# Bank pairs, joined sums and a second group by sevens in a two-layer hybrid block kernel

## The chip, the cores and the metric

One core of a Trainium2 chip runs the kernel. The metric is the device time of one execution in microseconds (us), the median of several runs.

## The reference

A network of two layers works on 256 tokens of width 2048, all in float32. Each layer has a mixer and a gated feed-forward part with 5632 hidden columns; a last normalisation ends it.

```python
def swiglu(hn, w_gate, w_up, w_down):
    return (jax.nn.silu(hn @ w_gate) * (hn @ w_up)) @ w_down

def reference(x, ...):
    h = x
    for layer in range(DEPTH):
        if layer % 2 == 0:
            h = h + gdn_rglru_mixer(rmsnorm(h, ab_norm[j]), ...)
        else:
            h = h + fox_moba_mixer(rmsnorm(h, cd_norm[j]), ...)
        h = h + swiglu(rmsnorm(h, ffn_norm[layer]), ffn_w_gate[layer], ffn_w_up[layer], ffn_w_down[layer])
    return rmsnorm(h, final_norm)
```

The change touches the two feed-forward parts and the places where they meet the mixers and the last normalisation.

## The kernel before

**Products in three.** Every float32 operand is split into a high half (a cast on ScalarE, L179 for weights, L376 for sums of weights) and a low half (a subtraction on VectorE, L180 and L377), and a product is three matmuls: high by high, low by high, high by low (`Bank.add`, L409 to L411; `xstat`, L303 to L305). A matmul has 128 tokens as its stationary side and 512 output columns. X is the transposed input of a stage, `hid` the transposed hidden tiles, both kept as two halves.

**Blocks.** `block()` computes two groups of 512 output columns (i = 0, 1) for two token halves (t = 0, 1) into four PSUM banks `F[t][i]`. The depth is walked in groups of four k-tiles of 128. A group is done plainly, in 48 matmuls with four weight units of 128x1024, or "by sevens" (`seven()`, Strassen's scheme with Winograd's sums): seven products of six matmuls, 42 in all, on sums of the weights (`total()`, L384, split by `halves()`) and on combinations of the input (`combine()`, tile `comb`). Four of the seven go into four banks M, and `ends()` (L460 to L465) adds those up into four tiles `e`, which are added to F at the block's end. Products by sevens are spread between the plain ones.

**Feed-forward.** `ffn()` goes through the eleven pairs of gate and up columns in pieces of four, four and three blocks. A gate and up block ends with `e <- F, e` sums (L529, L533), a Silu on ScalarE (L530) and a scaled product on VectorE (L534). `turn()` transposes such hidden tiles inside the next block (`Ph`, L503) and splits them into `hid` (L507, L508). After each piece come two down blocks (p = 0, 1) on `hid`, whose results go into the residual `h` (L554, L561). Gate and up blocks do two groups by sevens, except the first of each layer, which does none; the down blocks of the pieces of four do one for p = 0 and two for p = 1, those of the piece of three one each. A `hooks` table names the work that is put in at a plain product's number: the transposes, the combinations, a norm.

**Seams.** `phase()` opens the SBUF pools of a stage. The PSUM pools `acc` (four tiles of one bank; `Px` of the mixers and `F` share it) and `msp` (four tiles; `M`, transposes `Pt`, `Ph`) are opened once. A mixer ends with `out_proj()`, which adds `Px` to `h` (L359) and transposes it to X (`to_x()`, L326 to L328); the second mixer starts with projections `Px` on X by `xstat()`. The last block of the program sums up under `fin` (L557): `second_half()` takes the four `add` calls, sums of squares on ScalarE (L317), means (L1159), a root (L1164) and rates (L1168 to L1170), and writes the output; there VectorE's and ScalarE's order is as written. Elsewhere the scheduler sets it from the program's order and from the tiles' dependences. Each engine works through its own instructions in order.

## Time and profile before

| | |
|---|---|
| runs | 2228.13, 2226.42, 2227.39 us; median 2227.39 |
| profiled execution | 2228.4 us, span 2226.6 us |
| TensorE clock granted | 0.999 of full |
| TensorE busy | 2211.8 us, 99% |
| VectorE busy | 1917.1 us, 86% |
| ScalarE busy | 1284.9 us, 58% |
| GpSimd busy | 50.6 us, 2% |
| feed-forward of layer 0 | from 432 to 1128 us |
| feed-forward of layer 1 | from 1525 us to the end |

Matmuls are pipelined: one takes 0.39 us from start to end, and the next one starts well before that end. So the pitch of a row of matmuls is read from their starts. The same holds on VectorE in part: a new instruction starts a little before the last one ends.

### The profile page before, as it was taken

The page shows a single profiled execution, that of the slowest core. Times are in us where ns is not written, and L with a number is a line of the kernel's source. Part 1 is how long each engine was busy: PE and PEld are TensorE (multiplying, and loading weights), DVE is VectorE, ACT ScalarE, POOL GpSimd, SP SyncE. Part 2 cuts the span into 40 slices and gives each one's busy share as a digit, 9 for nine tenths or more (in the row PEclk, how much of TensorE's full clock was granted, in tenths as well). Part 3 has the DMA queues.
Part 4 walks back from the last instruction along what each step waited for, and adds up shares of the span by engine and source line. Part 5 has one row for each costly group of instructions (what it writes and reads, how often), then busy time and mean ns, then how long its engine had stood idle before and what let it go on. Part 6 is the DMA issues. An engine that isn't in the chain of part 4 may idle for free.

```text
span 2226.6 us, 30372 instructions
## 1 busy us (share of the span) xinstructions
PE 2211.8 (99%) x11002; PEld 1847.0 (83%) x11002; DVE 1917.1 (86%) x2713; ACT 1284.9 (58%) x1687; POOL 50.6 (2%) x62
## 2 busy tenths in 40 slices
PE   9999999999999999999999999999999999999998
PEld 8888888888888888888878888888888888888886
DVE  8899676679999999999966658866999999999998
ACT  6776664555555665555654444545665566555565
POOL 0000000000000000000000000000000000000000
PEclk9999999999999999999999999999999999999999
DMA  7445445677777776777665455556777777777774
GB/s 281 155 146 163 141 152 184 208 223 227 212 227 231 220 233 211 225 230 225 193 196 171 161 169 175 168 178 185 223 226 216 221 225 238 219 214 239 218 236 151
DMA packets 125992, 451.67 MB, mean 203 GB/s; under 512 B 14065, under 2 KB 15601, under 8 KB 125713
## 3 DMA queue, kind: packets, MB, share of 16 engines
q1 hardware_dynamic: 117488, 420.10, 58.3%
q0 software_dynamic: 8064, 29.36, 7.8%
q8 instruction: 86, 1.41, 0.3%
q14 instruction: 66, 0.53, 0.1%
q10 hardware_dynamic: 288, 0.27, 0.0%
HBM read 447.58 MB, written 2.10 MB: 202 GB/s over the span
## 4 chain that ended last, share of the span: by engine, by line
PE 95%; DVE 2%; issue 1%; ACT 1%; DMA 1%; DVEq 0%; ACTq 0%
PE F L411 15%; PE F L410 15%; PE F L409 15%; PE Pw L199 10%; PE Pw L204 5%; PE Px L303 5%; PE Px L304 5%; PE Px L305 5%; PE M L410 5%; PE M L411 4%; PE M L409 4%; PE Ph L503 1%; DVE wlo L180 1%; PE Psc L1068 1%; PE Pt L326 0%
## 5 line engine op out<-in xcount | busy, mean ns | idle before, releaser
L179 ACT CAST whi<-raw 128x1024 fp32r<-128x1024 f32 x720 | 755.3, 1051 | 666.8 <-PE F L411 263.8
L180 DVE TENSOR_TENSOR wlo<-raw,whi 128x1024 fp32r<-128x1024 f32 x720 | 874.5, 1219 | 189.3 <-PE Px L304 70.1
L199 PE MATMUL Pw<-X,whi 128*128 128x512 f32 x1088 | 388.3, 400 | 0.0
L409 PE MATMUL F<-whi,X 128*128 128x512 f32 x848 | 331.4, 391 | 0.0
L410 PE MATMUL F<-wlo,X 128*128 128x512 f32 x848 | 330.4, 390 | 0.0
L411 PE MATMUL F<-whi,X 128*128 128x512 f32 x848 | 330.0, 389 | 0.0
L204 PE MATMUL Pw<-X,wlo 128*128 128x256 f32 x1088 | 304.8, 280 | 1.0 <-DVE wlo L180 0.9
L376 ACT CAST thi<-T 128x1024 fp32r<-128x1024 f32 x168 | 176.6, 1051 | 124.1 <-DVE T L384 84.0
L199 PEld LDWEIGHTS Pw<-X,whi 128*128 128x128 f32 x1088 | 204.2, 188 | 47.7 <-issue 0.5
L377 DVE TENSOR_TENSOR tlo<-T,thi 128x1024 fp32r<-128x1024 f32 x168 | 205.1, 1221 | 28.0 <-ACT thi L376 27.3
L204 PEld LDWEIGHTS Pw<-X,wlo 128*128 128x128 f32 x1088 | 205.3, 189 | 2.4 <-DVE wlo L180 2.0
L409 PE MATMUL F<-whi,hid 128*128 128x512 f32 x480 | 187.5, 391 | 0.0
L411 PE MATMUL F<-whi,hid 128*128 128x512 f32 x480 | 186.9, 389 | 0.0
L410 PE MATMUL F<-wlo,hid 128*128 128x512 f32 x480 | 186.8, 389 | 0.0
L411 PEld LDWEIGHTS F<-whi,X 128*128 128x128 f32 x848 | 159.2, 188 | 33.1
L409 PEld LDWEIGHTS F<-whi,X 128*128 128x128 f32 x848 | 159.2, 188 | 32.7
L410 PEld LDWEIGHTS F<-wlo,X 128*128 128x128 f32 x848 | 159.2, 188 | 32.4
L384 DVE TENSOR_TENSOR T<-T,raw 128x1024 f32<-128x1024 f32 x112 | 136.5, 1219 | 1.1 <-DMA raw<-in_gu 0.2
L410 PE MATMUL M<-tlo,comb 128*128 128x512 f32 x336 | 131.8, 392 | 1.1 <-DVE tlo L377 1.0
L409 PE MATMUL M<-thi,comb 128*128 128x512 f32 x336 | 131.4, 391 | 0.0
L411 PE MATMUL M<-thi,comb 128*128 128x512 f32 x336 | 130.9, 390 | 0.0
L411 PEld LDWEIGHTS F<-whi,hid 128*128 128x128 f32 x480 | 90.1, 188 | 18.8
(389 smaller groups left out, 3409.5 us busy)
## 6 DMA issues: line engine op xcount, KB each, us to landing
raw<-in_gu SPq DMA_DIRECT2D x352, 512.0 KB, 4.4
raw<-in_dn SPq DMA_DIRECT2D x176, 512.0 KB, 4.4
raw<-in_w0w SPq DMA_DIRECT2D x72, 512.0 KB, 3.6
raw<-in_wo SPq DMA_DIRECT2D x64, 512.0 KB, 3.6
raw<-in_w1w SPq DMA_DIRECT2D x64, 512.0 KB, 3.6
raw<-in_gu POOLq DMA_DIRECT2D x40, 512.0 KB, 6.8
raw<-in_w1x SPq DMA_DIRECT2D x32, 512.0 KB, 3.7
raw<-in_w0x SPq DMA_DIRECT2D x16, 512.0 KB, 3.6
```

Of the source, the lines that this page charges most:

```text
L179: S.copy(hi, raw)
L180: V.tensor_sub(lo, raw, hi.bitcast(F32))
L199: PE.matmul(P.rearrange("p a b -> p (a b)"), hi[:, kk], X[:, k].rearrange("p a b -> p (a b)"), start=k == 0, stop=False)
L204: PE.matmul(P[:, 0], lo[:, kk], X[:, k, 0], start=False, stop=k == NK - 1)
L303: PE.matmul(Ps[t], x[:, 0, ts], hi[:, kk], start=k == 0, stop=False)
L304: PE.matmul(Ps[t], x[:, 0, ts], lo[:, kk], start=False, stop=False)
L376: S.copy(hi, t)
L377: V.tensor_sub(lo, t, hi.bitcast(F32))
L384: V.tensor_tensor(out=t, in0=a, in1=b, op=ALU.add)
L409: PE.matmul(self.t, xh, hi[:, kk], start=self.i == kk == 0, stop=False)
L410: PE.matmul(self.t, xh, lo[:, kk], start=False, stop=False)
L411: PE.matmul(self.t, xl, hi[:, kk], start=False, stop=kk == 1 and self.i == self.n - 1)
```

## The change

- `acc` becomes a pool of each phase: four tiles of one bank in a mixer, two tiles of two banks in a feed-forward part. `block()` takes one such pair for each column group i, with the two token halves as its two banks.
- `e` is one tile of four times 512 columns. The sums over it are joined to 1024 columns where two lie side by side or at a stride: two of the sums in `ends()`, gate and up sums, the product of gate and up, sums into `h`. Signs in `combine()` and `ends()` are chosen so that only sums are left behind.
- The up columns are scaled by ScalarE (a copy with a scale), and VectorE multiplies both halves in one instruction.
- `combine()` for hidden tiles takes a float32 copy that ScalarE makes of the transposed tile (`cf`), in place of adding up the two halves on VectorE; these combinations are put into gate and up blocks (number 6).
- First down blocks (p = 0) of the pieces of four do two groups by sevens, not one. `lead` there goes back to 2.

```diff
@@ body, phase @@
-    acc = pool("acc", 4, space=PSUM)
     msp = pool("msp", 4, space=PSUM)
-    mx, ogp, fp = Phase(), Phase(), Phase()
+    mx, ogp, fp, acc = Phase(), Phase(), Phase(), Phase()
...
+        acc.pool = st.enter_context(tc.tile_pool(name="acc", bufs=4 if mixer else 2, space=PSUM))
         ogp.pool = sub("og" if mixer else "hid", 3 if mixer else 1)
@@ combine @@
-    def combine(x4):
-
-        f = mx.tile([128, 4, T], F32, name="cf", tag="T", bufs=2)
+    def whole():
+
+        return mx.tile([128, 4, T], F32, name="cf", tag="T", bufs=2)
+
+    def combine(f):
+
...
-        V.tensor_tensor(out=f, in0=x4[:, :, 0].bitcast(F32), in1=x4[:, :, 1].bitcast(F32), op=ALU.add)
...
+    def combine_x(x4):
+
+        f = whole()
+        V.tensor_tensor(out=f, in0=x4[:, :, 0].bitcast(F32), in1=x4[:, :, 1].bitcast(F32), op=ALU.add)
+        return combine(f)
@@ sums, block, ends @@
-        return [[mx.tile([128, 512], F32, name=f"e{t}{i}", tag=f"e{t}{i}", bufs=1) for i in range(2)] for t in range(2)]
+        return mx.tile([128, 4, 512], F32, name="e", tag="e", bufs=1)
...
-        F = [[Bank(acc.tile([128, 512], F32, name=f"F{t}{i}", tag="acc"), n + (ns if t * i == 0 else 0)) for i in range(2)]
-             for t in range(2)]
+        P = [acc.tile([128, 2, 512], F32, name=f"F{i}", tag="acc") for i in range(2)]
+        F = [[Bank(P[i][:, t], n + (ns if t * i == 0 else 0)) for i in range(2)] for t in range(2)]
...
-            (c1, w5), (v, w7) = sums()
-            S.copy(c1, M[0].t)
-            for o, a, b, op in ((v, M[2], c1, ALU.subtract), (w5, M[1], v, ALU.add), (v, M[3], v, ALU.add), (w7, M[3], w5, ALU.add)):
-                V.tensor_tensor(out=o, in0=a.t, in1=b, op=op)
-            return [[c1, w5], [v, w7]]
+            e = sums()
+            S.copy(e[:, 0], M[0].t)
+            V.tensor_tensor(out=e[:, 1], in0=M[2].t, in1=e[:, 0], op=ALU.add)
+            V.tensor_tensor(out=e[:, 2], in0=M[3].t, in1=e[:, 1], op=ALU.add)
+            V.tensor_tensor(out=e[:, 1::2], in0=M[1].t.rearrange("p (a n) -> p a n", a=1).to_broadcast([128, 2, 512]),
+                            in1=e[:, 1:3], op=ALU.subtract)
+            return e
@@ ffn @@
+            if j < wanted[0]:
+
+                cf[j] = whole()
+                for t, (P, d) in enumerate(Ps):
+                    S.copy(cf[j][:, :, t * 128:(t + 1) * 128], P)
...
-            late = {4: lambda hid=hid: ch.update({0: combine(hid[:, 0:4])})}
+            wanted[0] = piece - 2
+            chs = lambda m: lambda: ch.update({m: combine(cf.pop(m))})
...
-                if j == 1 and piece == 3:
-
-                    hooks[6] = late[4]
+                if 0 < j <= wanted[0]:
+                    hooks[6] = chs(j - 1)
...
+                if e is not None:
+                    V.tensor_tensor(out=a[:, 0::2], in0=F[0], in1=a[:, 0::2], op=ALU.add)
                 for t in range(2):
-                    if e:
-                        V.tensor_tensor(out=a[t][0], in0=F[t][0], in1=e[t][0], op=(ALU.add, ALU.subtract)[t])
-                    S.activation(a[t][0], a[t][0] if e else F[t][0], AF.Silu, scale=nrm["rs"][:, t:t + 1])
+                    S.activation(a[:, 2 * t], F[0][:, t] if e is None else a[:, 2 * t], AF.Silu, scale=nrm["rs"][:, t:t + 1])
+                if e is not None:
+                    V.tensor_tensor(out=a[:, 1::2], in0=F[1], in1=a[:, 1::2], op=ALU.add)
                 for t in range(2):
-                    if e:
-                        V.tensor_tensor(out=a[t][1], in0=F[t][1], in1=e[t][1], op=ALU.add)
-                    V.scalar_tensor_tensor(out=a[t][0], in0=a[t][1] if e else F[t][1], scalar=nrm["rs"][:, t:t + 1],
-                                           in1=a[t][0], op0=ALU.mult, op1=ALU.mult)
+                    S.activation(a[:, 2 * t + 1], F[1][:, t] if e is None else a[:, 2 * t + 1], AF.Copy, scale=nrm["rs"][:, t:t + 1])
+                V.tensor_tensor(out=a[:, 0::2], in0=a[:, 1::2], in1=a[:, 0::2], op=ALU.mult)
...
-                if p == 0 and piece == 4:
-                    hooks.update(late)
-
-                    hooks[9] = lambda hid=hid: ch.update({1: combine(hid[:, 4:8])})
...
-                last = (3, 1, 3) if end and fin else (0, 5 if 4 in hooks else 2)
+                last = (3, 1, 3) if end and fin else ()
                 F, e = block(lambda i, u: dn[2 * p + i, u0 + u], lambda k: hid[:, k],
-                             {m: lambda m=m: ch[m] for m in range(1 + (p == 1 and piece == 4))}, piece, hooks, *last)
+                             {m: lambda m=m: ch[m] for m in range(piece - 2)}, piece, hooks, *last)
...
-                        fin(lambda t, i: V.tensor_tensor(out=hs[t][i], in0=F[t][i], in1=e[t][i], op=ALU.add))
+                        fin(lambda t, i: V.tensor_tensor(out=hs[i][:, t], in0=F[i][:, t], in1=e[:, 2 * t + i], op=ALU.add))
                     continue
-                for t in range(2):
-                    for i in range(2):
-                        V.tensor_tensor(out=hs[t][i], in0=F[t][i], in1=e[t][i], op=ALU.add)
+                for i in range(2):
+                    V.tensor_tensor(out=hs[i], in0=F[i], in1=e[:, i::2], op=ALU.add)
```

The order of the built program, at three places. A row is a line of the kernel, the operation, its output and inputs, its shape; "x4" is four alike in a row. Lines below are those of the program before and of the changed one, which differ by one at the seams and by up to 15 behind.

TensorE where layer 0's mixer hands over to its feed-forward part (Px is the end of the projection, Pt a transpose of the residual, F a bank, or a pair of banks, of the first block). Before:

```order
L305 MATMUL Px_4505<-whi,Od 128x512
L409 MATMUL F_4636<-whi,X 128x512
L326 MATMUL Pt<-tab,h 128x128 x4
L410 MATMUL F_4636<-wlo,X 128x512
L411 MATMUL F_4636<-whi,X 128x512
L409 MATMUL F_4636<-whi,X 128x512
L410 MATMUL F_4636<-wlo,X 128x512
L411 MATMUL F_4636<-whi,X 128x512
L409 MATMUL F_4638<-whi,X 128x512
L326 MATMUL Pt<-tab,h 128x128 x4
L410 MATMUL F_4638<-wlo,X 128x512
```

The same place in the change:

```order
L306 MATMUL Px_4505<-whi,Od 128x512
L327 MATMUL Pt<-tab,h 128x128 x8
L418 MATMUL F_4640<-whi,X 128x512
L419 MATMUL F_4640<-wlo,X 128x512
L420 MATMUL F_4640<-whi,X 128x512
```

The seven matmuls of F that stood ahead of the second four transposes stand behind them now. Layer 1 has the same at its own seam.

TensorE where layer 0's feed-forward part hands over to the second mixer, with the engines that each instruction waits for (Px is the first projection). Before:

```order
L411 MATMUL F_10109<-whi,hid 128x512
L326 MATMUL Pt<-tab,h 128x128 [waits DVE_49] x2
L326 MATMUL Pt<-tab,h 128x128 x6
L303 MATMUL Px_10463<-whi,X 128x512 [waits Activation_49]
L304 MATMUL Px_10463<-wlo,X 128x512
```

The same place in the change:

```order
L420 MATMUL F_10014<-whi,hid 128x512
L327 MATMUL Pt<-tab,h 128x128 [waits DVE_49]
L327 MATMUL Pt<-tab,h 128x128 x5
L327 MATMUL Pt<-tab,h 128x128 [waits PE_49]
L327 MATMUL Pt<-tab,h 128x128
L304 MATMUL Px_10364<-whi,X 128x512 [waits DVE_49,Activation_49]
L305 MATMUL Px_10364<-wlo,X 128x512
```

The order of the matmuls is the same; the first of Px has got a wait for VectorE, which is the last joined sum into h (L575).

VectorE at the end of the program, with waits (h<-F is a last sum into the residual; fin holds the means and rates). Before:

```order
L554 TENSOR_TENSOR e_19606<-h,e_19606 128x512
L557 TENSOR_TENSOR h<-F_19440,e_19603 128x512 [waits PE_49]
L557 TENSOR_TENSOR h<-F_19441,e_19604 128x512 [waits DVE_49,PE_49]
L557 TENSOR_TENSOR h<-F_19442,e_19605 128x512 [waits PE_49]
L1159 SCALAR_TENSOR_TENSOR fin_13967<-ssp,fin_13963 128x1 [waits Activation_49]
L1159 SCALAR_TENSOR_TENSOR fin_13965<-ssp,fin_13967 128x1 [waits DVE_49,Activation_49]
L1168 RECIPROCAL fin_13967<-fin_13966 128x1 [waits DVE_49,Activation_49]
L1169 SCALAR_TENSOR_TENSOR fin_13966<-fin_13965,fin_13967,fin_13966 128x1 [waits DVE_49]
L1170 RECIPROCAL fin_13966<-fin_13966 128x1 [waits DVE_49]
L557 TENSOR_TENSOR h<-F_19443,e_19606 128x512 [waits PE_49]
```

The same place in the change:

```order
L568 TENSOR_TENSOR e<-h,e 128x1024
L572 TENSOR_TENSOR h<-F_19248,e 128x512 [waits DVE_49,PE_49]
L572 TENSOR_TENSOR h<-F_19249,e 128x512 [waits PE_49]
L572 TENSOR_TENSOR h<-F_19248,e 128x512 [waits DVE_49]
L1173 SCALAR_TENSOR_TENSOR fin_13869<-ssp,fin_13865 128x1 [waits Activation_49]
L1173 SCALAR_TENSOR_TENSOR fin_13867<-ssp,fin_13869 128x1 [waits DVE_49,Activation_49]
L1182 RECIPROCAL fin_13869<-fin_13868 128x1 [waits DVE_49,Activation_49]
L1183 SCALAR_TENSOR_TENSOR fin_13868<-fin_13867,fin_13869,fin_13868 128x1 [waits DVE_49]
L1184 RECIPROCAL fin_13868<-fin_13868 128x1 [waits DVE_49]
L572 TENSOR_TENSOR h<-F_19249,e 128x512
```

The order is the same. Before, each of the four sums waits for TensorE; now the first two do, each for the whole of its pair.

## Rows read from the trace of the kernel before

**Rows 1.** The page: span, and busy time of each engine.
```profile
span 2226.6 us, 30372 instructions
...
PE 2211.8 (99%) x11002; PEld 1847.0 (83%) x11002; DVE 1917.1 (86%) x2713; ACT 1284.9 (58%) x1687; POOL 50.6 (2%) x62
```
**Rows 2.** Windows: busy time of each engine in three stretches, granted clock, DMA share.
```profile
979.00:1020.70 41.70, 41.70 (x189) 34.60 (x188) 40.76 (x45) 24.71 (x28) 0.86 (x1) 1.00 0.73 219
...
400.00:1128.00 728.00, 727.16 (x3268) 600.32 (x3267) 674.11 (x725) 427.37 (x485) 24.32 (x28) 1.00 0.73 219
1541.00:2218.00 677.00, 676.57 (x3021) 557.96 (x3019) 632.30 (x661) 393.85 (x424) 24.17 (x28) 1.00 0.73 218
```
**Rows 3.** Waits of TensorE from 395 to 2218 us: total, times, longest.
```profile
PE M L410 <- DVE tlo L377: 1.0, 2, 0.8
```
**Rows 4.** Timeline, TensorE, first and last of the final seven matmuls: start, duration.
```profile
2216.13 0.39 PE L411 MATMUL F<-whi,hid 128*128 128x512 f32 x1
...
2217.49 0.39 PE L411 MATMUL F<-whi,hid 128*128 128x512 f32 x1
```
**Rows 5.** Groups by line, VectorE, 400 to 1128 us: busy, mean ns, idle before.
```profile
L180 DVE TENSOR_TENSOR wlo<-raw,whi 128x1024 fp32r<-128x1024 f32 x247 | 299.3, 1219 | 23.8 <-PE F L410 9.2 <-PE Px L304 5.2 <-ACT junk L317 2.7
...
L464 DVE TENSOR_TENSOR e<-M,e 128x512 f32<-128x512 f32 x64 | 42.5, 684 | 2.2 <-PE M L411 1.9
```
**Rows 6.** Groups by line, ScalarE, 400 to 1128 us.
```profile
L376 ACT CAST thi<-T 128x1024 fp32r<-128x1024 f32 x84 | 88.3, 1051 | 59.6 <-DVE T L384 35.7 <-PE F L410 14.4 <-PE F L411 8.1
...
L462 ACT COPY e<-M 128x512 f32<-128x512 f32 x16 | 9.3, 580 | 0.3 <-PE M L411 0.3
```
**Rows 7.** Timeline, TensorE, mixer to feed-forward in layer 0.
```profile
432.41 0.39 PE L409 MATMUL F<-whi,X 128*128 128x512 f32 x1
432.68 0.66 PE L326 MATMUL Pt<-tab,h 128*128 128x128 f32 x4
433.09 0.47 PE L410 MATMUL F<-wlo,X 128*128 128x512 f32 x1
...
434.32 0.40 PE L409 MATMUL F<-whi,X 128*128 128x512 f32 x1
434.56 0.60 PE L326 MATMUL Pt<-tab,h 128*128 128x128 f32 x4
```
**Rows 8.** Timeline, VectorE, the same place.
```profile
432.54 1.22 DVE L180 TENSOR_TENSOR wlo<-raw,whi 128x1024 fp32r<-128x1024 f32 x1
433.67 0.69 DVE L359 TENSOR_TENSOR h<-Px,h 128x512 f32<-128x512 f32 x1
```
**Rows 9.** Timeline, TensorE, mixer to feed-forward in layer 1.
```profile
1524.55 0.39 PE L409 MATMUL F<-whi,X 128*128 128x512 f32 x1
...
1526.69 0.60 PE L326 MATMUL Pt<-tab,h 128*128 128x128 f32 x4
```
**Rows 10.** Timeline, TensorE, feed-forward of layer 0 to the second mixer.
```profile
1127.87 0.39 PE L411 MATMUL F<-whi,hid 128*128 128x512 f32 x1
...
1128.89 0.48 PE L303 MATMUL Px<-whi,X 128*128 128x512 f32 x1
```
**Rows 11.** Timeline, VectorE, the same place.
```profile
1128.12 1.23 DVE L180 TENSOR_TENSOR wlo<-raw,whi 128x1024 fp32r<-128x1024 f32 x1 [0.35 <-ACT junk L317]
1129.27 0.68 DVE L561 TENSOR_TENSOR h<-F,e 128x512 f32<-128x512 f32 x1
```
**Rows 12.** Timeline, VectorE, the end of the program.
```profile
2213.84 0.69 DVE L557 TENSOR_TENSOR h<-F,e 128x512 f32<-128x512 f32 x1 [0.92 <-PE F L411]
...
2215.81 0.42 DVE L1159 SCALAR_TENSOR_TENSOR fin<-ssp,fin 128x1 f32<-128x1 f32 x2
...
2216.83 0.16 DVE L1170 RECIPROCAL fin<-fin 128x1 f32<-128x1 f32 x1
2217.92 0.69 DVE L557 TENSOR_TENSOR h<-F,e 128x512 f32<-128x512 f32 x1 [0.92 <-PE F L411]
```
**Rows 13.** Timeline, ScalarE, the end of the program.
```profile
2215.16 0.19 ACT L317 ACTIVATION_READ_ACCUMULATOR junk<-h 128x1 f32 x1
```

More of the change, by code (lines that the diff above doesn't have):

```diff
@@ L385, in total @@
         return t, halves(t)
-    def combine(x4):
-        f = mx.tile([128, 4, T], F32, name="cf", tag="T", bufs=2)
+    def whole():
+        return mx.tile([128, 4, T], F32, name="cf", tag="T", bufs=2)
+    def combine(f):
         c = mx.tile([128, 4, 2, 128], F32, name="cc4", tag="T", bufs=2)
         r = fp.tile([128, 2, 4, 2, 128], F32R, name="comb", tag="comb", bufs=4)
-        V.tensor_tensor(out=f, in0=x4[:, :, 0].bitcast(F32), in1=x4[:, :, 1].bitcast(F32), op=ALU.add)
         a11, a21, a12, a22 = (f[:, 2 * j:2 * j + 2, t * 128:(t + 1) * 128] for j in range(2) for t in range(2))
-        for i, (x, y) in enumerate(((a21, a22), (a21, a11), (a22, c[:, 1]), (a12, c[:, 2]))):
-            V.tensor_tensor(out=c[:, i], in0=x, in1=y, op=ALU.subtract)
+        for i, x, y, op in ((0, a21, a22, ALU.subtract), (1, a11, a21, ALU.subtract), (2, c[:, 0], a11, ALU.subtract), (3, a12, c[:, 2], ALU.add)):
+            V.tensor_tensor(out=c[:, i], in0=x, in1=y, op=op)
         S.copy(r[:, 0], c)
@@ L490, in block @@
                     e = ends()
-        return [[y.t for y in f] for f in F], e
+        return P, e
     def ffn(L, then, fin=None):
         gu, dn = A[f"gu{L}"], A[f"dn{L}"]
-        todo, cx, ch = [], {}, {}
+        todo, cx, ch, cf = [], {}, {}, {}
         def turn():
@@ L508, in turn @@
                 V.tensor_tensor(out=d[:, :, 1], in0=P, in1=d[:, :, 0].bitcast(F32), op=ALU.subtract)
-        b = 0
+            if j < wanted[0]:
+                cf[j] = whole()
+                for t, (P, d) in enumerate(Ps):
+                    S.copy(cf[j][:, :, t * 128:(t + 1) * 128], P)
+        b, wanted = 0, [0]
         for groups in ((0, 2, 2, 2), (2, 2, 2, 2), (2, 2, 2)):
@@ L518, in ffn @@
                 if b == 0:
-                    hooks[5] = lambda: cx.update({0: combine(X[:, 0:4])})
+                    hooks[5] = lambda: cx.update({0: combine_x(X[:, 0:4])})
                     hooks[8] = rstd
-                    hooks[10] = lambda: cx.update({1: combine(X[:, 4:8])})
-                if j == 1 and piece == 3:
-                    hooks[6] = late[4]
+                    hooks[10] = lambda: cx.update({1: combine_x(X[:, 4:8])})
+                if 0 < j <= wanted[0]:
+                    hooks[6] = chs(j - 1)
                 F, e = block(lambda i, u: gu[b, u, i], lambda k: X[:, k], {m: lambda m=m: cx[m] for m in range(groups[j])}, 4, hooks)
-                a = e or sums()
+                a = sums() if e is None else e
+                if e is not None:
+                    V.tensor_tensor(out=a[:, 0::2], in0=F[0], in1=a[:, 0::2], op=ALU.add)
                 for t in range(2):
-                    if e:
-                        V.tensor_tensor(out=a[t][0], in0=F[t][0], in1=e[t][0], op=(ALU.add, ALU.subtract)[t])
-                    S.activation(a[t][0], a[t][0] if e else F[t][0], AF.Silu, scale=nrm["rs"][:, t:t + 1])
+                    S.activation(a[:, 2 * t], F[0][:, t] if e is None else a[:, 2 * t], AF.Silu, scale=nrm["rs"][:, t:t + 1])
+                if e is not None:
+                    V.tensor_tensor(out=a[:, 1::2], in0=F[1], in1=a[:, 1::2], op=ALU.add)
                 for t in range(2):
-                    if e:
-                        V.tensor_tensor(out=a[t][1], in0=F[t][1], in1=e[t][1], op=ALU.add)
-                    V.scalar_tensor_tensor(out=a[t][0], in0=a[t][1] if e else F[t][1], scalar=nrm["rs"][:, t:t + 1],
-                                           in1=a[t][0], op0=ALU.mult, op1=ALU.mult)
-                    todo.append((hid, j, t, a[t][0]))
+                    S.activation(a[:, 2 * t + 1], F[1][:, t] if e is None else a[:, 2 * t + 1], AF.Copy, scale=nrm["rs"][:, t:t + 1])
+                V.tensor_tensor(out=a[:, 0::2], in0=a[:, 1::2], in1=a[:, 0::2], op=ALU.mult)
+                for t in range(2):
+                    todo.append((hid, j, t, a[:, 2 * t]))
                 b += 1
```

7 lines of the change are left out of this document (4 added, 3 removed).

## The prediction

> **What bounds the kernel now.** I read the page's busy shares first, then the windows view of the two feed-forward stretches, the waits of TensorE there, and last, row by row, the places where one stage hands over to the next. TensorE is busy for 2211.8 of 2226.6 us [rows 1], at a granted clock of 1.00 all through [rows 2]. In the feed-forward stretches the windows leave 728.00 − 727.16 = 0.84 and 677.00 − 676.57 = 0.43 us of TensorE idle [rows 2], and its waits view has one kind of entry, 1.0 us in two times, for a low half of a weight sum [rows 3]. So within those stretches the time is the number of matmuls by their pitch: seven matmuls in a row start 1.36 us apart over six steps, 1.36 / 6 = 0.2267 us each [rows 4]. VectorE is busy for 674.11 of those 728 us [rows 2]: close behind, but not the limit. What TensorE does not do is the end of the program (from the last matmul's start at 2217.49 [rows 4] to 2226.6 [rows 1]) and little else. A change is then worth the matmuls it takes out, less every place where TensorE has to stand still that it did not before.
>
> Durations below are from the profiled execution, 2228.4 us, of which 2226.6 are its span; that is 1.0 us above the median of the three runs, 2227.39. I add the sum to both. About 0.2%, 4.45 us here, is what a measurement of this kernel can tell from no change: the bounds are 2222.9 and 2231.8.
>
> **Matmuls removed.** A group of four k-tiles costs 4 × 12 = 48 matmuls when done plainly and 7 × 6 = 42 by sevens. A second group by sevens in the first down block of the two pieces of four, in both layers, is 4 × 6 = 24 matmuls: 24 × 0.2267 = **−5.4 us**, all of it on the engine that bounds.
>
> **VectorE and ScalarE in the blocks: 0.** A sum of two 512 columns takes 0.684 us each on VectorE [rows 5], and 1024 columns take 1.219 [rows 5]; joining saves 2 × 0.684 − 1.219 = 0.15 us of busy time per pair, some 140 pairs, 21 us. The adds of hid's two halves (10 × 1.22 [rows 5]) go too. Against it stand three more splits and three more weight totals in each of the four new groups, 24 × 1.219 = 29 us. This comes out near even, so VectorE stays under TensorE. ScalarE takes over the scaling of the up columns and the copies of the transposed hidden tiles, 64 more instructions of about 0.58 us [rows 6], and 16 − 4 = 12 more casts of 1.051 us: it is busy for 427 of 728 us [rows 2] and has the room. The tightest kind of block exists already: the one from 979.00 to 1020.70 makes a combination of hid inside a gate and up block, with VectorE busy 40.76 of 41.70 us, and TensorE is busy for all 41.70 [rows 2]. The change has five such blocks a layer in place of one, each without the add that the copies replace. Each new group also reads one block of weights a second time, by an accumulating transfer from GpSimd's queue, four in all; the DMA engines are at 0.73 [rows 2] and SP's queue issues what it did. I cost all that at nothing; if the cover goes, the first rival has the price. Since 1.27 us is all the idle time there is to win in these stretches [rows 2], the lower end of this term is −1.3.
>
> **Bank pairs inside a layer: 0, but with little left over.** Before, the next block's first matmul on a bank needs one sum of 512 columns to be done. Now it needs the joined sum over both token halves, which can't start before the second half's last matmul. From that matmul to the next use of the pair are 13 matmuls, 13 × 0.2267 = 2.95 us. A sum starts 0.43 us after its last matmul at best (2217.49 [rows 4] to 2217.92 [rows 12]) and takes 1.22: 1.30 us to spare. At 13 places a weight split which waits for the last matmul but one stands directly before the sum on VectorE. Such a split takes 433.67 − 432.54 = 1.13 us from start to start [rows 8], so the sum starts at −0.23 + 0.43 + 1.13 = 1.33 and ends at 2.55 us: 0.39 us to spare. No stall follows as long as VectorE's operands are there in time.
>
> **Mixer to feed-forward, twice: +3.2.** Here the pools matter. Before, the four banks of one pool serve both stages, so TensorE runs one matmul of the first block at 432.41, four transposes at 432.68, and six more matmuls from 433.09 to 434.32, while VectorE works through a split and the second sum into h; then come the other four transposes at 434.56 [rows 7]. Those seven matmuls fill the wait for the sum that starts at 433.67 and takes 0.69 [rows 8]. In the change the order puts all eight transposes directly behind the projection, and the first block behind them, since its banks belong to a pool that is opened with the stage. The order of VectorE there is as before. The second four transposes still wait for the same sum, and nothing covers it: 7 × 0.2267 = 1.59 us. The other seam has the same rows, 1524.55 to 1526.69 [rows 9], so 2 × 1.59 = 3.2. By the matmul pitch alone it can't be much more, and a gain is excluded: no instruction leaves.
>
> **Feed-forward to second mixer: +1.5.** Before, the last matmul of the block starts at 1127.87 and the first of the new projection at 1128.89, behind eight transposes [rows 10], with no wait on VectorE. In the change that matmul waits for VectorE: its bank lies under the last pair, so the joined sum into h has to be done. If that sum goes as soon as it may, it ends at 1127.87 + 0.43 + 1.22 = 1129.52, 0.6 us late. But on VectorE it stands behind a weight split, whose like starts at 1128.12 before, with the next sum at 1129.27 [rows 11]; from there it ends at 1130.49, 1.6 us late. The split is in the order of the change as well, so I take 1.5, nearer to the upper end.
>
> What the row shows is that a longer sum at a seam holds TensorE for its whole length. The Trainium skill, "Perfetto Trace Analysis", section "Optimizing Scalar/DVE Operations", says that grouping improves throughput if the engine is saturated, and that, where it is not but causes bubbles on other engines, breaking up instructions may let work finish sooner. By its first half the joins would be a gain everywhere, which is the third rival; by its second half these seams lose, and the waits that the order shows agree.
>
> **The tail: +2.6.** Call the last matmul's start L, 2217.49 [rows 4]. Before, the four last sums wait each for its own bank: the second runs at 2213.84, the means and the first token half's rate from 2215.81 to 2216.99 (2216.83 + 0.16), and only the fourth waits for L, at L + 0.43 [rows 12]. In the change two banks are one tile, and the order has a wait on TensorE at the first two sums only: the second sum, of token half 0, waits for the pair's last matmul, which is L. So it starts at L + 0.43 instead of 3.65 us before L. Then what used to lie under matmuls lies behind them: the sum of squares on ScalarE is read 2215.16 + 0.19 − 2213.84 = 1.51 us after that sum's start [rows 12, 13], so means start at about L + 2.0; they and the rate take 2216.99 − 2215.81 = 1.18 [rows 12]; the fourth sum stands behind them on VectorE and starts at about L + 3.1. From it on the program is the same. 3.1 − 0.43 = 2.67, less some for overlaps: 2.6. If VectorE's third sum or the root on ScalarE goes quicker it is 2.2, if they queue 3.0.
>
> **Sum.** −5.4 + 0 + 0 + 3.2 + 1.5 + 2.6 = +1.8 us (in hundredths −5.44 + 3.17 + 1.5 + 2.6 = 1.83): 2230.2 for the profiled execution, **2229.2** by the median. With each term at its own bounds (blocks −1.3 to +1, seam 0.6 to 1.6, tail 2.2 to 3.0) the case runs from 2226.6 to 2230.7.
>
> **Rivals.**
> *Late casts (slower).* In the ten blocks with a combination from copies, ScalarE's copies wait in its queue for VectorE's low half of hid and for a free buffer, and casts of weights stand behind them. VectorE already waits for casts there, 40.76 of 41.70 us leave it 0.94 [rows 2]. One cast of 1.051 us [rows 6] late before the up sum overruns the 0.39 us by 0.66. Six of the 13 tight places lie in those blocks, the other four have about 0.95 to spare and lose 0.1: 6 × 0.66 + 4 × 0.1 = 4.4, so 2229.2 + 4.4 = 2233.6. It decides from 0.83 us of delay at each of the six (then 2.6 us are lost in all). For it speaks that VectorE has no room there; against it, that the block at 979 runs without a stall.
> *The seams cost nothing (no change).* If the order at the seams is made good by work behind it, for instance because the next weights were late anyway, only the tail is left: 2227.39 − 5.44 + 2.6 = 2224.6. Against it: TensorE is busy right through those places now [rows 7, 9], so nothing was late.
> *The joins pay and no new wait shows (faster).* Then 24 matmuls and all idle time of the stretches go: 2227.39 − 5.44 − 1.27 = 2220.7. It needs the waits at the seams and the tail, which are in the order, to be short.
>
> **Chances.** Forecast 0.55, late casts 0.20, seams free 0.15, all free 0.10. The range reaches to 2224.4 and 2234.2, which takes in the second rival and the first with a little over. Faster by over 0.2%: the third rival, 0.10. Slower by over 0.2%: the first rival and the upper end of the forecast, if two of its bounds meet, 0.23. No change: 0.67.
>
> **What would show it.** Seven matmuls fewer between transposes, and TensorE idle for about 1.5 us ahead of the second four transposes, at both seams; a wait of TensorE for the sum into h of 1 to 2 us at the start of the second mixer; the last sum into h about 3 us after the last matmul's start. From the first block to the last of each layer TensorE should be idle as little as before and have 12 matmuls less per layer. Waits of a pair's first matmul for the sums of the gate or up columns would mean the first rival. A last sum at 0.4 us after the last matmul would prove the tail wrong.

## The result and the profile after

The changed kernel takes 2241.87 us (median of five runs, 2240.73 to 2246.91) against 2227.39: **slower by 14.5 us**, a ratio of 1.0070 with a 95% interval of 1.0057 to 1.0082. The forecast was 2229.2 with a range up to 2234.2. The page of its profiled execution, as [rows 1]:

```profile
span 2239.0 us, 30278 instructions
...
PE 2212.6 (99%) x10978; PEld 1840.3 (82%) x10978; DVE 1921.3 (86%) x2587; ACT 1333.4 (60%) x1763; POOL 54.0 (2%) x66
```

TensorE has 24 instructions less and is busy as long as before. Its waits from 395 us on, as [rows 3] (total, times, longest):

```profile
PE M L419 <- DVE tlo L378: 3.1, 4, 1.2
PE F L418 <- DVE e L545: 2.5, 2, 1.3
PE Pt L327 <- DVE h L360: 2.2, 2, 1.1
PE F L418 <- DVE h L575: 1.7, 2, 0.9
PE Px L304 <- DVE h L575: 1.5, 1, 1.5
```

One kind of entry has become five. The third and the fifth are the seams; the first, second and fourth lie inside the blocks. The second and the fourth are new in kind: the first matmul on a pair of banks waits for a joined sum over that pair, 2.5 + 1.7 = 4.2 us in all. The timeline of TensorE at the first seam, as [rows 7]:

```profile
430.39 0.39 PE L306 MATMUL Px<-whi,Od 128*128 128x512 f32 x1
430.89 0.66 PE L327 MATMUL Pt<-tab,h 128*128 128x128 f32 x4
432.62 0.66 PE L327 MATMUL Pt<-tab,h 128*128 128x128 f32 x4 [1.08 <-DVE h L360]
433.03 0.47 PE L418 MATMUL F<-whi,X 128*128 128x512 f32 x1
```

The second four transposes wait for the sum into h, with nothing in between. From the last Px to the start of the 30th matmul of the block it is 9.34 us, before 7.82, and 9.31 against 7.83 in layer 1: +1.5 each. At the second mixer (timeline of TensorE, as [rows 10], and of VectorE, as [rows 11]):

```profile
1131.07 0.39 PE L420 MATMUL F<-whi,hid 128*128 128x512 f32 x1
1131.30 1.03 PE L327 MATMUL Pt<-tab,h 128*128 128x128 f32 x8
1133.83 0.47 PE L304 MATMUL Px<-whi,X 128*128 128x512 f32 x1 [1.50 <-DVE h L575]
```

```profile
1131.32 1.23 DVE L181 TENSOR_TENSOR wlo<-raw,whi 128x1024 fp32r<-128x1024 f32 x1
1132.46 1.22 DVE L575 TENSOR_TENSOR h<-F,e 128x1024 f32<-128x1024 f32 x1
```

The joined sum stands behind the split and ends at 1133.68; the 30th matmul of Px comes 10.36 us after the last F, before 8.74: +1.6. The tail on VectorE, as [rows 12] (the last matmul starts at 2227.46):

```profile
2227.89 1.29 DVE L572 TENSOR_TENSOR h<-F,e 128x512 f32<-128x512 f32 x2 [2.03 <-PE F L420]
...
2230.21 0.16 DVE L1184 RECIPROCAL fin<-fin 128x1 f32<-128x1 f32 x1
2230.29 0.67 DVE L572 TENSOR_TENSOR h<-F,e 128x512 f32<-128x512 f32 x1
```

The last sum starts 2.83 us after the last matmul, before 0.43, and the span ends 11.5 us after it, before 9.1: +2.4.

These three make 3.0 + 1.6 + 2.4 = 7.0 us, and 24 matmuls less make −5.4. The rest is in the blocks. I call **loss** what the starts of neighbouring matmuls in a block lie further apart than the pitch of 0.2267 us, added up over the 17 blocks of each layer: 7.7 us before (4.1 and 3.6), 20.4 now (10.5 and 9.9). A gap ahead of the next block's first matmul counts with the block that ends. So 7.0 − 5.4 + 12.7 = 14.3, the 14.5 measured. (The two spans differ by 12.4, since this execution came to the last Px of layer 0 at 430.39 instead of 432.18, in a stage with the same instructions.)

More than half of the 12.7 lies in **one block, the first gate and up block of the second piece**: 0.4 and 0.7 us before, 4.0 and 3.6 now (layers 0 and 1). VectorE there in layer 0, now:

```profile
694.97 1.22 DVE L385 TENSOR_TENSOR T<-raw,raw 128x1024 f32<-128x1024 f32 x1
696.11 1.22 DVE L385 TENSOR_TENSOR T<-T,raw 128x1024 f32<-128x1024 f32 x1
697.24 2.35 DVE L181 TENSOR_TENSOR wlo<-raw,whi 128x1024 fp32r<-128x1024 f32 x2
699.51 1.22 DVE L378 TENSOR_TENSOR tlo<-T,thi 128x1024 fp32r<-128x1024 f32 x1
700.67 1.23 DVE L378 TENSOR_TENSOR tlo<-raw,thi 128x1024 fp32r<-128x1024 f32 x1
705.21 1.23 DVE L181 TENSOR_TENSOR wlo<-raw,whi 128x1024 fp32r<-128x1024 f32 x1 [3.31 <-ACT whi L180]
```

It stands still for 3.31 us, in which the cast that it waits for waits for a weight (ScalarE's timeline):

```profile
704.12 2.00 ACT L180 CAST whi<-raw 128x1024 fp32r<-128x1024 f32 x2 [3.48 <-DMA raw<-in_gu]
```

SP's and GpSimd's queues tell why it is late:

```profile
692.69 0.39 SPq L174 DMA_DIRECT2D raw<-in_gu  x1
...
697.39 0.33 SPq L174 DMA_DIRECT2D raw<-in_gu  x1
```

```profile
696.72 0.86 POOL L452 DMA_DIRECT2D raw<-in_gu  x1 [17.10 <-DMA raw<-in_gu]
```

SP issues nothing for 4.7 us: the next load goes into a buffer that the total at 696.11 still reads, until 696.11 + 1.22 = 697.33. It is the load that the cast waits for, so it took 704.12 − 697.39 = 6.7 us, and it runs together with an accumulating transfer that started 0.67 us ahead. The windows view has the engines' side; now, and before:

```profile
696.00:700.00 4.00, 4.00 (x19) 3.32 (x18) 4.00 (x5) 2.04 (x3) 0.86 (x1) 1.00 0.43 100
700.00:704.10 4.10, 4.10 (x19) 3.35 (x18) 1.90 (x2) 0.64 (x1) 0.00 (x0) 1.00 1.01 299
```

```profile
696.00:700.00 4.00, 4.00 (x19) 3.31 (x18) 3.95 (x4) 2.11 (x2) 0.00 (x0) 1.00 0.76 261
700.00:704.10 4.10, 4.10 (x20) 3.17 (x19) 3.18 (x4) 2.36 (x3) 0.86 (x1) 1.00 0.72 193
```

The DMA engines are busy for 0.43 of the first stretch (100 GB/s) and for all of the second (1.01), where before they had an even 0.76 and 0.72. TensorE, still fed, feels it later: stalls of 0.6, 1.4 and 1.4 us behind the matmuls at 707.5, 718.0 and 728.8, while VectorE works without a pause from 708 to 720 and doesn't catch up. The third is the next block's first matmul, which waits for the joined gate sum (TensorE, then VectorE):

```profile
730.43 0.47 PE L418 MATMUL F<-whi,X 128*128 128x512 f32 x1 [1.23 <-DVE e L545]
```

```profile
729.06 1.22 DVE L545 TENSOR_TENSOR e<-F,e 128x1024 f32<-128x1024 f32 x1
```

### The profile page after: what moved, and what is told of

It reads as the page before. It is cut to its first block, busy times and chain, and to the rows that moved or that the text cites. A ratio compares the mean times of both kernels' runs of the same rounds, so it can differ in the third digit from the quotient of the medians.

```text
span 2239.0 us, 30278 instructions
## 1 busy us (share of the span) xinstructions
PE 2212.6 (99%) x10978; PEld 1840.3 (82%) x10978; DVE 1921.3 (86%) x2587; ACT 1333.4 (60%) x1763; POOL 54.0 (2%) x66
## 5 line engine op out<-in xcount | busy, mean ns | idle before, releaser
L377 ACT CAST thi<-T 128x1024 fp32r<-128x1024 f32 x180 | 189.2, 1051 | 148.9 <-DVE T L385 119.1
L378 DVE TENSOR_TENSOR tlo<-T,thi 128x1024 fp32r<-128x1024 f32 x180 | 219.7, 1221 | 30.3 <-ACT thi L377 29.0
L418 PE MATMUL F<-whi,hid 128*128 128x512 f32 x424 | 166.2, 392 | 1.7 <-DVE h L575 1.7
L420 PE MATMUL F<-whi,hid 128*128 128x512 f32 x424 | 165.3, 390 | 0.0
L419 PE MATMUL F<-wlo,hid 128*128 128x512 f32 x424 | 165.2, 390 | 0.0
L385 DVE TENSOR_TENSOR T<-T,raw 128x1024 f32<-128x1024 f32 x120 | 146.3, 1219 | 2.1 <-DMA raw<-in_gu 1.2
L419 PE MATMUL M<-tlo,comb 128*128 128x512 f32 x360 | 141.9, 394 | 3.1 <-DVE tlo L378 3.1
L418 PE MATMUL M<-thi,comb 128*128 128x512 f32 x360 | 141.9, 394 | 0.0
L420 PE MATMUL M<-thi,comb 128*128 128x512 f32 x360 | 140.2, 390 | 0.0
L418 PEld LDWEIGHTS F<-whi,hid 128*128 128x128 f32 x424 | 79.6, 188 | 19.5 <-DVE h L575 3.3
```

Source lines behind the costliest of these rows:

```text
L377: S.copy(hi, t)
L378: V.tensor_sub(lo, t, hi.bitcast(F32))
L385: V.tensor_tensor(out=t, in0=a, in1=b, op=ALU.add)
L418: PE.matmul(self.t, xh, hi[:, kk], start=self.i == kk == 0, stop=False)
L419: PE.matmul(self.t, xh, lo[:, kk], start=False, stop=False)
L420: PE.matmul(self.t, xl, hi[:, kk], start=False, stop=kk == 1 and self.i == self.n - 1)
```

## The experiments

The table has every run: the median, the loss in both layers' blocks, and that of the first gate and up block of the second piece (layers 0 and 1).

| run | what it is | median us | loss us | that block us |
|---|---|---|---|---|
| before | | 2227.4 | 7.7 | 0.4, 0.7 |
| after | the change | 2241.9 | 20.4 | 4.0, 3.6 |
| r1 | moved combinations from copies, second sevens; single banks | 2245.4 | 30.4 | 3.6, 3.6 |
| r2 | pairs and copies, one seven | 2246.5 | 18.9 | 3.6, 3.9 |
| r3 | moved combinations from copies | 2239.9 | 22.1 | 0.1, 0.1 |
| r4 | pairs, joins, up scale only | 2247.9 | 19.9 | 3.8, 4.1 |
| r5 | after, combinations without low halves | 2244.4 | 26.8 | 4.5, 3.9 |
| r6 | r5 with nine weight buffers | 2238.6 | 18.4 | 0.3, 0.3 |
| r7 | r5 with three sum buffers | 2245.9 | 24.3 | 4.2, 3.9 |
| r8 | before without those halves, nine buffers | 2234.3 | 14.9 | 0.2, 0.2 |
| r9 | before, loads dealt with a shift of 1 | 2228.8 | 10.1 | 0.5, 0.7 |
| r10 | before, shift of 3 | 2234.6 | 15.7 | 0.3, 0.2 |
| r11 | moved combinations and second sevens | 2254.6 | 40.3 | 4.8, 4.4 |
| r12 | after, shift of 1 | 2249.1 | 27.1 | 2.3, 2.1 |
| r13 | bare pairs only | 2238.9 | 10.6 | 0.4, 0.4 |
| r14 | moved combinations | 2239.6 | 18.3 | 0.1, 0.1 |
| r15 | after, shift of 5 | 2239.8 | 19.2 | 0.2, 0.1 |
| r16 | after, shift of 3 | 2245.9 | 24.1 | 1.9, 1.7 |
| r17 | after, less other work on VectorE | 2237.7 | 14.1 | 0.8, 0.8 |
| r18 | after, fewer low halves on VectorE | 2239.9 | 18.9 | 1.9, 1.9 |

The loss is that of the one profiled execution. The medians follow from it: 2227.4 + (loss − 7.7), −5.4 with the second groups by sevens, +7.0 with pairs, gives every run within 2 us but r17 (2.3 off) and r5 (3.7 off; its profiled execution, 2249.6, was the longest of its four). Executions of one changed kernel lie up to 8.6 us apart (r5), those of r1 from 2242.3 to 2250.8, so 3 or 4 us between two medians can be chance.

**Which part costs (r1 to r4).** Edits to the changed kernel: r1 puts back the single banks, `e` as four tiles, the sums of 512 columns and VectorE's scaled product; r2 is

```diff
-                             {m: lambda m=m: ch[m] for m in range(piece - 2)}, ...
+                             {m: lambda m=m: ch[m] for m in range(piece - 2 if p else 1)}, ...
```

r3 does both, and r4 is r2 with `late` and its hooks 4 and 9 of the kernel before in place of `chs`. Two small things of the change stay in some of them: in r1 to r4, `ends()` adds up M[1] last and not second; in r1 to r3, the products by sevens of a first down block start at its second plain product, not at the fifth (`lead` is 2). Neither was tried by itself.

> The change with its bank pairs, joined sums and up scale on ScalarE undone: four banks of one pool, sums of 512 columns, VectorE's scaled product; the combinations from copies and the second groups by sevens stay. Theory A (pairs and joined sums make all the new waits, inside the blocks too): the seams, the tail and the blocks are as before, and 24 matmuls are gone: 2227.4 - 5.4 = 2222.0 us. Theory B (the second groups by sevens starve VectorE of weights inside the blocks, some 12 us): 2222.0 + 12.4 = 2234.4. Theory C (the copies, which hold one of two sum buffers and queue ahead of casts, cost the 12 us): 2234.4 as well.

> The change with one group by sevens in each first down block, as before it; pairs, joined sums and copies stay. Theory A (pairs and joined sums): 2241.9 + 5.4 = 2247.3 us. Theory B (second groups by sevens): only seams and tail stay, 2227.4 + 6.9 = 2234.3. Theory C (copies): 2227.4 + 6.9 + 12.4 = 2246.7.

> Only the combinations from ScalarE's copies, placed in gate and up blocks; single banks, sums of 512 columns, one group by sevens in each first down block. Theory A and theory B: as before, 2227.4 us. Theory C (copies): 2227.4 + 12.4 = 2239.8.

> Only the bank pairs, the joined sums and the up scale on ScalarE; combinations from hid's halves at the places of before, one group by sevens in each first down block. Theory A (pairs and joined sums): 2227.4 + 6.9 + 12.4 = 2246.7 us. Theory B and theory C: seams and tail alone, 2227.4 + 6.9 = 2234.3.

Measured 2245.4, 2246.5, 2239.9 and 2247.9. Theory B falls by r3 and r4: both lose 12 to 14 us more in the blocks than the kernel before, with no second seven in first down blocks. So does theory A by r3 and r1, and theory C by r4. The parts don't add up: by the medians the second groups by sevens win 4.6 us on top of pairs and copies (r2 to the change), and lose 5.5 on top of copies alone (r3 to r1). Single banks undo seams and tail (in r1 the second mixer's 30th Px stands at 8.72, the end at 9.1, as before), and yet r1 isn't faster than the change: its blocks lose 10.0 us more, which takes back the 7.0. Its median is 3.5 us higher, but the executions overlap (2242.3 to 2250.8 against 2240.7 to 2246.9). The waits of TensorE in r1:

```profile
PE M L418 <- DVE tlo L377: 4.0, 4, 1.5
PE M L417 <- ACT thi L376: 3.5, 5, 1.2
```

**Buffers (r5 to r8).** The low halves of the combinations give way to two more weight buffers (r6, r8) or a third sum buffer (r7):

```diff
-        r = fp.tile([128, 2, 4, 2, 128], F32R, name="comb", tag="comb", bufs=4)
+        r = fp.tile([128, 4, 2, 128], F32R, name="comb", tag="comb", bufs=4)
...
-        if more and loads[0] > 0 and loads[0] % 7 in (1, 3, 5, 6):
-            raw = mx.tile([128, 1024], F32, name="raw4", tag="raw4", bufs=4)
+        if more and loads[0] > 0 and loads[0] % 9 in (1, 2, 4, 5, 7, 8):
+            raw = mx.tile([128, 1024], F32, name="raw4", tag="raw4", bufs=6)
```

> A control for the next runs: the change with the low halves of the combinations left out (their subtraction overwrites the high half in place, and both matmuls read that one tile), which frees 16 KB per partition; so the combinations differ from the reference's. The same instructions on every engine. All theories: as the change, 2241.9 us, up to 2 more, since the first matmul on a combination now waits for VectorE and not for ScalarE alone.

> The control (combinations without low halves) with nine weight buffers in place of seven. Theory E (the blocks' stalls come from the ring of seven weight buffers: one stays held while its accumulating transfer runs and until the last of the seven products, and the loads behind it in SP's queue come late): nearly all of the 12 us inside the blocks go, 2230 to 2233. Theory F (two buffers for sums of weights, one held by a copy of hidden tiles): as the control, 2242. Theory G (the order and the length of VectorE's instructions at the block ends): as the control, 2242.

> The control (combinations without low halves) with three buffers for sums and copies in place of two. Theory E (weight ring): as the control, 2242 us. Theory F (sum buffers): 2230 to 2236. Theory G (order and length on VectorE): 2242.

> The kernel before with the low halves of the combinations left out in the same way and nine weight buffers. Theory E (weight ring): TensorE has 7.8 us of gaps above its pitch in the feed-forward blocks of the kernel before; with more buffers some of them go, 2221 to 2227. Theories F and G: 2227 to 2229.

Measured 2244.4, 2238.6, 2245.9 and 2234.3. Theory F falls by r7, theory G by r6. Theory E holds for the block shown above: 4.5 and 3.9 us become 0.3 and 0.3. VectorE's waits there (686 to 735 us), in r5:

```profile
DVE wlo L181 <- ACT whi L180: 3.0, 1, 3.0
DVE T L385 <- DMA raw<-in_gu: 2.6, 1, 2.6
DVE tlo L378 <- ACT thi L377: 0.7, 1, 0.7
```

and in r6:

```profile
DVE tlo L378 <- ACT thi L377: 1.6, 3, 0.6
DVE e L545 <- PE F L420: 0.2, 1, 0.2
DVE wlo L181 <- PE F L419: 0.2, 1, 0.2
```

But it doesn't hold for the whole: four first down blocks now lose 1.6 to 2.1 us each, so 18.4 us are left of r5's 26.8, and r6 misses the 2230 to 2233 that theory E had. The kernel before gets slower in r8, not faster; r8 has the low halves left out as well as nine buffers, and no run has the kernel before with the first alone, so which of the two costs isn't shown.

**The fit of the ring, and second sevens without pairs and copies (r9 to r12).** r9, r10, r12 (and r15, r16) differ by one line:

```diff
-        if more and loads[0] > 0 and loads[0] % 7 in (1, 3, 5, 6):
+        if more and loads[0] > 0 and (loads[0] + 1) % 7 in (1, 3, 5, 6):
```

r11 is r1 with `combine_x(hid[:, 4 * m:4 * m + 4])` in place of the copies.

> The kernel before with the pattern that deals the weight loads of a feed-forward part to the ring of three and the ring of four buffers shifted by one load. No instruction is added, taken away or made longer. Theory H (VectorE at 94% of TensorE's time leaves no room in the blocks, and the kernel before is fitted to the order in which buffers come free; any other fit costs 5 to 20 us, whatever the edit): 2232 to 2247 us. Theories C (the copies cost by themselves) and A (the pairs cost by themselves): 2227 to 2229.

> The same with a shift by three loads. Theory H (fit): 2232 to 2247 us, and another number than the shift by one. Theories A and C: 2227 to 2229.

> Only the second groups by sevens in the first down blocks, with the combinations made from hid's halves on VectorE, as before, but in the gate and up blocks; single banks and sums of 512 columns. Theory A (pairs) and theory C (copies): 2227.4 - 5.4 = 2222.0 us, or up to 2 more for the added sums on VectorE. Theory B (second groups by sevens) and theory H (fit): 2234 or more.

> The changed kernel with the dealing of weight loads shifted by one load, nothing else. Theory H (fit): off from 2241.9 by several us, up or down; if the place of the stalls moves with the shift, that speaks for it too. Theories A and C: 2241.9, with the stalls in the same blocks.

Measured 2228.8 (ratio 1.0004, 0.9994 to 1.0013), 2234.6, 2254.6 and 2249.1. The kernel before, timed beside them, took 2228.25. A shift that adds no instruction costs the kernel before nothing or 6.3 us, and the changed one 6.4 (20.9 over the kernel before, not 14.5): theory H is right that the fit alone is worth as much as the 5.4 us that the change was to win, and wrong that any other fit costs. The place of the stalls moves too: in r12 the first gate and up block of the second piece loses 2.3 and 2.1 us, and the last block of layer 1 loses 6.1 in place of 0.4. r11 is the dearest: 24 matmuls less and 32.6 us more loss. On it the copies win 9.2 us (r1); with one seven they win nothing (r14 to r3, below).

**Pairs or joins, copies or the move (r13 to r16).** r13 is the kernel before with these lines only; r14 is r11 with one seven in first down blocks, as in r2.

```diff
-    acc = pool("acc", 4, space=PSUM)
+        acc.pool = st.enter_context(tc.tile_pool(name="acc", bufs=4 if mixer else 2, space=PSUM))
...
+        P = [acc.tile([128, 2, 512], F32, name=f"F{i}", tag="acc") for i in range(2)]
+        F = [[Bank(P[i][:, t], n + (ns if t * i == 0 else 0)) for i in range(2)] for t in range(2)]
```

> The kernel before with nothing but the bank pairs and the pools of a phase: every sum stays at 512 columns, VectorE's scaled product stays, and so do the combinations and the groups by sevens. Theory I (the pairs alone, by the dependence of a tile of two banks): seams, tail and the 3.8 us in the first gate and up block of the second piece, 2227.4 + 6.9 + 8 = 2242 us. Theory J (the joined sums move two totals ahead of a weight split on VectorE in that block, and so a load): that block loses under 1 us, as before, and only seams and tail are left, 2227.4 + 6.9 = 2234.3.

> The kernel before with the combinations of hidden tiles moved into gate and up blocks, made from hid's halves as before; no copies, no second group by sevens in the first down blocks, no pairs. Theory K (the move into blocks with two groups by sevens, not the copies, is what costs in the run with copies only): 2240 us or more, with losses in the second and the last but one gate and up block of a piece. Theory C (the copies): 2227 to 2229.

> The changed kernel with the dealing of weight loads shifted by five loads, a try for a better fit. Theory H (fit): another number than 2241.9 and 2249.1, and the loss of 3.6 to 4.0 us in the first gate and up block of the second piece gone or in another block. If the fit is all there is inside the blocks, it could go down to 2230; it can't come under 2227 without the seams and the tail.

> The same with a shift by three loads. Theory H: another number again, 2230 to 2250 us, and the loss in another block.

Measured 2238.9, 2239.6, 2239.8 and 2245.9. **r13**: the loss is 10.6, and the block in question loses 0.4 as before, so theory I falls and theory J holds there, though the whole is 4.6 us over J's 2234.3. The tile of two banks doesn't bring the 3.8 of that block in r4; what r4 has besides does: the joined sums with their new order, and the up scale on ScalarE. VectorE's waits in it (686 to 735 us), r13:

```profile
DVE tlo L377 <- ACT thi L376: 1.7, 2, 1.0
DVE wlo L180 <- ACT whi L179: 0.9, 1, 0.9
```

and r4 (690 to 735 us):

```profile
DVE wlo L181 <- ACT whi L180: 3.2, 1, 3.2
DVE T L385 <- DMA raw<-in_gu: 1.8, 1, 1.8
```

What r13 has left is mostly the price of the pairs at the seams and the tail, 7.8 us of its 11.5 by the same readings as above; another 1.5 is one wait for the sums of squares ahead of the last block of layer 1. TensorE's waits of r13:

```profile
PE Pt L326 <- DVE h L359: 2.2, 2, 1.1
PE F L409 <- ACT junk L317: 1.5, 1, 1.5
PE Px L303 <- ACT X L327: 1.5, 1, 1.5
```

**r14** is as slow as r3, so ScalarE's copies aren't what costs there. The move of the combinations into blocks with two groups by sevens is the likely cause of its 10.6 us of loss, but not shown alone, since r14 also has the order in `ends()` and the `lead` of first down blocks that r1 and r3 have. Against these two speaks that r4, with the first of them, loses 0.2 to 0.5 us in the last gate and up blocks of the pieces of four, and that r14's own first down blocks lose 0.1 to 0.3. Theory K had the time, but not the places: r14 loses most in those last gate and up blocks (2.9 and 1.7 us in layer 0, 1.2 and 1.3 in layer 1), which have no combination, and 0.1 to 1.0 in the blocks that have one. **r15** has the same order on VectorE in the block in question as the change and no stall there, since the dealing lets the late weight's load go at 693.29 instead of 697.39; yet other blocks lose 1 to 1.6 us each, and only 2 us are won, which is within the spread. Most of this is waits of a pair's first matmul for a joined sum into h: 6.4 us in seven times, where the change has 1.7 in two. So the stall in the block in question hangs on both, the order on VectorE and the buffer that a load gets, and the pairs then lose elsewhere.

**Room on VectorE (r17, r18).**

```diff
-                V.tensor_tensor(out=a[:, 0::2], in0=a[:, 1::2], in1=a[:, 0::2], op=ALU.mult)
...
-                    V.tensor_tensor(out=et, in0=h[:, t, c], in1=et, op=ALU.add)
```

```diff
-            M[3].add(cx(1), halves(b12))
+            hi = fp.tile([128, 1024], F32R, name="thi", tag="thi", bufs=2)
+            S.copy(hi, b12)
+            M[3].add(cx(1), (hi, hi))
```

> The changed kernel with work of VectorE left out that touches no weight: the product of gate and up (silu of the gate goes on alone) and the sum of the residual into the down blocks' sums; 22 + 22 instructions of 1024 columns, 50 us of VectorE in all. TensorE's instructions stay. Theory H (VectorE is too full to make up for a late weight): the blocks' loss falls from 20 to about 8 us as before, 2241.9 - 12 = 2230. Theory E (the weight ring and the transfers' latency alone): 2239 to 2242.

> The changed kernel with the low half left out of one weight sum in four (the last product of each group by sevens reads its high half twice); 60 instructions of 1.13 us start to start, 68 us of VectorE. TensorE's and ScalarE's instructions stay. Theory H (VectorE too full): 2230 or less. Theory E (ring and latency): the buffer of that weight comes free some 1 us earlier, so 2236 to 2242.

Measured 2237.7 and 2239.9 (r17 leaves out 22 products and 24 sums). Theory H falls by both; theory E has r18's time (2236 to 2242), but not r17's (2239 to 2242), which lies between what the two expected. With some 50 us of VectorE's work gone, 6.3 of the 12.7 us of loss go; with some 68 gone, 1.5. So the amount of VectorE's work alone doesn't set the loss. In r17 TensorE's longest total is the wait of a block's first matmul for a joined sum, and in r18 it is the same wait, 5.1 us in ten times. In r17:

```profile
PE F L418 <- DVE e L545: 3.5, 5, 1.0
PE Pt L327 <- DVE h L360: 2.2, 2, 1.1
```

**What stays open.** No run brings the change's blocks back to 7.7 us. Three bundles of edits each make losses: joined sums with their order and the up scale (r13 to r4, 9.3 us of loss), combinations moved into gate and up blocks with the two small edits named above (r14, 10.6), and second groups by sevens on top of those (r14 to r11, 22.0; on top of pairs and copies only 1.5, r2 to the change). One place is followed to the end of its chain. How the rest of the 12.7 us divides isn't settled, and can't be by sums, since the parts act on each other. The parts of a bundle weren't tried apart. No version of these beats the kernel before.

## Why the prediction was wrong

- **Matmuls, −5.4: right.** 24 less, at the same pitch.
- **Mixer to feed-forward, +3.2: right**, 3.0 measured. Transposes in a row and 1.1 us of waiting for the sum, as the order had it.
- **Feed-forward to second mixer, +1.5: right**, 1.6. The sum stood behind the split, the upper of the two cases.
- **The tail, +2.6: right**, 2.4. The last sum came at 2.83 us after the last matmul, not 3.1.
- **"VectorE and ScalarE in the blocks: 0" is the step that failed**, and with it the condition of the next one, "as long as VectorE's operands are there in time". Together with the bank pairs, the next point, they measured +12.7 us. The sum of VectorE's work was right: it comes out even, 1299.9 us before and 1297.4 now in the two feed-forward stretches (though a join saves 0.07 us from start to start, 2 × 0.60 − 1.13, and not the 0.15 of the busy times). But I took an even sum for an even flow. The block at 979, which I named as the tight one, loses 0.4 us in the change, 0.1 before; the one that loses 4.0 has no combination in it at all. I had looked for instructions added to a block, and not at what a new order of the old ones does to the buffers of the weights, whose loads SP issues one after the other as VectorE lets go of them. r13 against r4 shows it for the joined sums with the up scale; for the moved combinations r14 makes it likely. Why the blocks with stalls are those and no others stays open but for the one followed above.
- **"Bank pairs inside a layer: 0, but with little left over" failed too.** The first matmul on a pair waits for a joined sum in four places, 2.5 + 1.7 = 4.2 us, which are part of the 12.7. The 0.39 us to spare held only if VectorE was on time, and its lateness ate them: at 730.43 behind the late weight. The sum into h of the first down block in the second piece stood behind two joined sums of the residual and a split, so it started 3.1 us after the last matmul on its pair (899.01 against 895.95), not 1.3. In r15 such waits come to 6.4 us, in r18 to 5.1 + 1.3; in r13, with sums of 512 columns, to 0.7.
- **The range of this term, −1.3 to +1.** The lower end took TensorE's idle time for all there was to win. But a matmul counts as busy for 0.39 us and the next one starts 0.23 us behind it, so busy time hides gaps of up to 0.16: by starts the blocks lost 7.7 us before. The upper end had no row behind it. The rows gave a warning that I didn't take: VectorE had 0.94 us left in a block of 41.70 [rows 2], so 3.3 us of waiting in one block could not be made up in it.
- **The first rival (late casts, 2233.6)** had the right sign and a wrong place: VectorE did wait for a cast, but the cast waited for a transfer, and in another block. The sign that I had set for it, a pair's first matmul waiting for a gate or up sum, did come (2.5 us), so that sign doesn't tell this rival from a late weight. ScalarE's copies, its cause, cost nothing measurable by themselves (r3 against r14).
- **The seams cost nothing** and **the joins pay** are both out. That grouping can improve throughput where an engine is saturated (the Trainium skill, "Perfetto Trace Analysis", "Optimizing Scalar/DVE Operations") is borne out by busy time alone: in r4 VectorE is busy for 1282.0 us, 18 less than before, and yet r4 takes 9.0 us more than r13, which has the pairs without joins and up scale, and 20 more than the kernel before. On top of the second sevens the joined kernel has the lower median (the change against r1, 3.5 us), which isn't clear of the spread.

## What to carry to other kernels

When an engine that feeds the bound one is busy for 94% of its time, price an edit by what it does to the order in which buffers come free, block by block, and not by the sum of its instructions; an edit whose own rows say zero may cost more than every wait that can be read from the order. A slack of some tenths of a microsecond that holds only while that engine is on time is a cost, not a zero. Waits that do stand in the order, at the hand-over of two stages and at the end, can be worked out beforehand to within some tenths of a microsecond. Before a gain of a quarter per cent is hunted by moving work about, shift something that changes no work: here the dealing of loads alone was worth 0 to 6 us.

## What the hardware showed

The page's loads of gate and up weights, in the changed kernel (KB each, median us from issue to landing):

```profile
raw<-in_gu SPq DMA_DIRECT2D x352, 512.0 KB, 4.5
```

The one shown above took 6.7 us, beside an accumulating transfer. That goes for the whole program: the 67 loads of feed-forward weights that SP issued within 3 us behind an accumulating transfer took 6.4 us (median), the other 461 took 4.4; in the kernel before it is 6.8 us for 49 and 4.3 for 479. A pause on SP's queue by itself makes no load slower: the loads that followed one of over 3.5 us, without such a transfer, took 3.6 us. In the kernel before, the load that VectorE waited for in that block was issued at 698.44, ahead of the transfer at 700.08, and took 4.3 us.

A stall of TensorE for a late operand leaves a trail: behind the three stalls above, the next matmul starts 0.34, 0.34 and 0.31 us later instead of 0.23, which adds some 0.1 us to each. Gaps of this small kind, 30 to 200 ns above the pitch, add up to 4.6 us in the blocks before and 8.4 now; the trails of the longer stalls are 0.5 and 1.0 of that, and what makes the rest isn't shown.
